# A compressing MLP whose first layer swaps its matmul operands, in a fused hybrid decoder block

## The chip, the cores and the metric

The kernel runs on one core of a Trainium2 chip. A core has a matrix engine (TensorE: PE in the rows, its weight loads PEld), a vector engine (VectorE, DVE), a scalar engine with function tables (ScalarE, ACT), GpSimd (POOL) and a queue that issues most DMAs (SyncE, SP). The metric is device time of one execution in microseconds (us), smaller being better. Of the kernel before, three runs gave 804.38, 804.61 and 807.77 us, a median of 804.61.

## The reference, cut to what matters

One decoder layer on 512 tokens of width 1024, all in float32: a norm, one input projection, four token mixers side by side, gates, an output projection, and an MLP. The change lies in the second mixer, sparse attention, and there in the small MLP that compresses keys and values:

```python
n_cmp = (S - CMP_LEN) // CMP_STRIDE + 1        # 31 windows of 32 tokens, 16 apart
def compress(t, pe, w1, w2):                    # t: keys or values, 2 heads of 64
    blk = jnp.take(heads(t), cmp_idx, axis=1) + pe[None, None, :, None, :]
    blk = jnp.swapaxes(blk, 2, 3).reshape(B, n_cmp, N_KV_HEADS, CMP_LEN * HEAD_DIM)
    hid = jax.nn.gelu(jnp.einsum('bnhf,fe->bnhe', blk, w1))   # f = 2048, e = 128
    return jnp.einsum('bnhe,ed->bnhd', hid, w2)               # d = 64
k_cmp = _rms(compress(kc, cmp_pe[0], cmp_w1[0], cmp_w2[0]), k_g[0])
v_cmp = compress(vc, cmp_pe[1], cmp_w1[1], cmp_w2[1])
```

So the first layer multiplies 62 rows (31 windows of 2 heads) of 2048 numbers by a weight of 2048 x 128, once for keys and once for values. Queries attend to `k_cmp`; the scores also choose the blocks that are read in full, and `v_cmp` is summed with them.

## The kernel before, in words

Activations lie transposed, features on the 128 partitions and tokens along the free dimension. A product of large matrices is split in three passes of a rounded type (`mm3`, lines 84 to 86: high by high, low by high, high by low), so PE runs long rows of matmuls of 128 x 128 weights against 256 or 512 columns. ACT makes the high half of each weight (line 79), DVE the low half (line 80).

Small pieces of attention are generators, called tasks. `tick()` steps at most two of them after each few matmuls of a projection, so their instructions are recorded between the projection's. The recorded program then goes through a scheduler that reorders the instructions of each engine by an estimate of its own; hence an edit in one task can move instructions far from it. On the chip each engine works off its queue in the order that results.

`cmp_task(j, acc)` compresses keys (j = 0) and values (j = 1). It loads `w1_j0` and `w1_j1` (two tiles of 8 weight blocks of 128 x 128), gathers windows into `blk_j` (128 x 16 x 62), and multiplies at line 544 in plain float32, 16 matmuls into one PSUM tile `hid_j`. A plain float32 matmul is two records in the trace, each with a weight load of its own. The weight block stays in the array (the stationary operand) and 62 columns of `blk` stream past it, so `hid_j` comes out as 128 hidden features x 62 windows. ACT applies gelu from PSUM into `hT0` (line 552) or, twice, into `hT1` (line 577), padded to 32 windows a head. Line 555 (`kcmp`) and line 580 (`vcmp`) multiply by the second layer's weight. From `kcmp` a norm on DVE and ACT makes `kccat`, line 571 turns it (`kctr`), and all attention heads wait for it and for `vcmp`.

All of this stands between the projections named `kv` (keys and values of the window), `gv` and `gu` (inputs of the gated mixer). After the changed place, PE also runs in half-width form, with 64 of the array's columns, for `gm` (line 720) and `pv` (lines 671 and 675), two such products beside each other.

The other names that the rows show: `VL` is gelu of `gv` (line 699); `rsu_k` a square root in a key's norm (line 356); `TG` tanh of attention gates (line 586); `kcat` and `KTT` a key before and after its turn (lines 492 and 74); `ktr` that turn (line 508); `s` the scores (lines 635 and 640); `p` their exponentials (line 648); `sh` and `gt` projections. ACT has one set of function tables at a time; where the next function belongs to another set, an ACT_TABLE_LOAD stands before it.

Of the kernel before, what the change touches and what calls it, by code (L numbers as in the profile page):

```python
# [11 lines left out]
AF = mybir.ActivationFunctionType  # L12
# [4 lines left out]
P = 128  # L17
# [8 lines left out]
NCMP = 31  # L26
# [11 lines left out]
def block_kernel(ctx: ExitStack, tc: tile.TileContext, x, w_in, w_branch, w_gate, w_out,  # L38
                 w_mlp1, w_mlp2, cmp_w1, cmp_w2, ws_t, bs, smalls, rows, norm1_g, norm2_g, out):
    nc = tc.nc  # L40
# [15 lines left out]
    def ps(name, dt=F32):  # L56
        return psp.tile([P, 512], dt, tag="ps", name=name)
# [7 lines left out]
    def t4(name, shape, dt=F32):  # L65
        return br.tile(shape, dt, tag="t4", name=name, bufs=8)

    def f32(ap):
        return ap.bitcast(F32)
# [263 lines left out]
    def rsqrt(dst, src, scale, eps, name, eng=None):  # L333
        ve = eng or nc.vector
        pr, n = src.shape[0], src.shape[1]
        h = const.tile([P, 16], F32, tag="rs_h", name=f"rsh_{name}", bufs=2)[:pr, :n]
        t = const.tile([P, 16], F32, tag="rs_t", name=f"rst_{name}", bufs=2)[:pr, :n]
        nc.vector.tensor_scalar(out=h, in0=src, scalar1=scale, scalar2=eps, op0=ALU.mult, op1=ALU.add)
        nc.vector.tensor_scalar(out=dst.bitcast(I32), in0=h.bitcast(I32), scalar1=-0.5, scalar2=float(0x5F3759DF),
                                op0=ALU.mult, op1=ALU.add)  # L340
        ve.tensor_scalar_mul(h, h, -0.5)
        for _ in range(3):
            ve.tensor_tensor(out=t, in0=dst, in1=dst, op=ALU.mult)
            ve.tensor_tensor(out=t, in0=t, in1=h, op=ALU.mult)
            if eng is None:
                ve.scalar_tensor_tensor(out=dst, in0=t, scalar=1.5, in1=dst, op0=ALU.add, op1=ALU.mult)
            else:
                ve.tensor_scalar_add(t, t, 1.5)
                ve.tensor_tensor(out=dst, in0=dst, in1=t, op=ALU.mult)
# [30 lines left out]
    ident = const.tile([P, P], F32, name="ident")  # L380
# [139 lines left out]
    def cmp_task(j, acc):  # L520
        w1 = []
        for half in range(2):
            w = t4(f"w1_{j}{half}", [P, 8, P])
            nc.sync.dma_start(w, cmp_w1[j, half * 1024 : (half + 1) * 1024, :].rearrange("(k p) c -> p k c", p=P))
            w1.append(w)
        kc = t4(f"kc_{j}", [P, S])
        nc.scalar.copy(kc, acc)
        kc2 = t4(f"kc2_{j}", [P, 2, S])
        nc.gpsimd.dma_start(kc2[0:64, 1, :], kc[64:128, :])
        nc.gpsimd.dma_start(kc2[64:128, 0, 0:511], kc[0:64, 1:512])  # L530
        nc.vector.tensor_copy(kc2[0:64, 0, :], kc[0:64, :])
        nc.vector.tensor_copy(kc2[64:128, 1, 0:511], kc[64:128, 1:512])
        blk = t4(f"blk_{j}", [P, 16, 2, NCMP])
        pe = sm[:, O_PE + 16 * j : O_PE + 16 * j + 16]
        for h in range(2):
            base = kc2[:, h, :].rearrange("p (n s) -> p s n", s=16)
            for u in range(2):
                nc.vector.tensor_tensor(
                    out=blk[:, 8 * u : 8 * u + 8, h, :], in0=base[:, 0:16:2, u : u + NCMP],
                    in1=pe[:, 8 * u : 8 * u + 8].unsqueeze(2).to_broadcast([P, 8, NCMP]), op=ALU.add)  # L540
        yield 9
        hp_ = ps(f"hid_{j}")
        for lp in range(16):
            nc.tensor.matmul(hp_[:, :62], w1[lp // 8][:, lp % 8, :], blk[:, lp, :, :].rearrange("p h n -> p (h n)"),
                             start=lp == 0, stop=lp == 15)
            if lp % 4 == 3 and lp < 15:
                yield 0
        hv = hp_[:, :62].rearrange("p (h n) -> p h n", h=2)
        if j == 0:
            hT = att.tile([P, 2, 32], F32, name="hT0")  # L550
            nc.gpsimd.memset(hT, 0.0)
            nc.scalar.activation(out=hT[:, :, :NCMP], in_=hv, func=AF.Gelu_apprx_tanh)
            yield 1
            kp = ps("kcmp")
            nc.tensor.matmul(kp[:64, :HD], hT.rearrange("p h n -> p (h n)"), w2[:, 0, :], start=True, stop=True)
            kr = att.tile([64, HD], F32, name="kr")
            nc.scalar.copy(kr, kp[:64, :HD])
            sq = kp[:64, :HD]
            nc.vector.tensor_tensor(out=sq, in0=kr, in1=kr, op=ALU.mult)
            ss = att.tile([64, 1], F32, name="kss")  # L560
            nc.vector.tensor_reduce(out=ss, in_=sq, axis=AX.X, op=ALU.add)
            r = att.tile([64, 1], F32, name="krr")
            rsqrt(r, ss, 1.0 / HD, 1e-6, "kc")
            nc.vector.scalar_tensor_tensor(out=kr, in0=kr, scalar=r[:, 0:1], in1=row[:64, R_KG : R_KG + HD],
                                           op0=ALU.mult, op1=ALU.mult)
            kk = att.tile([64, 2, HD], F32R, name="kccat")
            nc.scalar.copy(kk[:, 0, :], kr)
            nc.vector.tensor_tensor(out=kk[:, 1, :], in0=kr, in1=f32(kk[:, 0, :]), op=ALU.subtract)
            yield 4
            pt = ps("kctr", F32R)  # L570
            nc.tensor.transpose(pt[:, :64], kk.rearrange("p a d -> p (a d)"), identr[:64, :64])
            nc.vector.tensor_copy(KCT, f32(pt[:, :64]))
        else:
            hT = att.tile([P, 2, 2, 32], F32, name="hT1")
            nc.gpsimd.memset(hT, 0.0)
            for dup_ in range(2):
                nc.scalar.activation(out=hT[:, :, dup_, :NCMP], in_=hv, func=AF.Gelu_apprx_tanh)
            yield 1
            vp = ps("vcmp")
            nc.tensor.matmul(vp[:, :HD], hT.rearrange("p a b n -> p (a b n)"), w2[:, 1, :], start=True, stop=True)  # L580
            for h in range(4):
                nc.vector.tensor_copy(VBD[32 * h : 32 * h + 32, h, :], vp[32 * h : 32 * h + 32, :HD])
# [315 lines left out]
    for j in range(2):  # L898
        proj_T("kc", lambda j, a: tcmp.append(Task(cmp_task(j, a))), j)
# [576 lines left out]
```

## Time and profile before

| what | value |
|---|---|
| median of three runs | 804.61 us (804.38 to 807.77) |
| profiled execution, whole | 805.33 us |
| its span, first to last instruction | 803.4 us |
| PE busy | 792.0 us, 99% of the span |
| DVE, ACT, POOL busy | 607.3, 398.2, 91.2 us |
| granted TensorE clock | 1.00 in every stretch |

The profiled execution takes 1.9 us around its span. A busy PE counts records that overlap each other, so for the pace of a row of matmuls one reads the starts of records, not their lengths. In the timeline a row is: start, busy length, engine, line, operation, out<-in, shape, count; in brackets the idle time before it and what ended it.

### The profile page before, as it was taken

The page shows a single profiled execution, that of the slowest core. Times are in us where ns is not written, and L with a number is a line of the kernel's source. Part 1 is how long each engine was busy: PE and PEld are TensorE (multiplying, and loading weights), DVE is VectorE, ACT ScalarE, POOL GpSimd, SP SyncE. Part 2 cuts the span into 40 slices and gives each one's busy share as a digit, 9 for nine tenths or more (in the row PEclk, how much of TensorE's full clock was granted, in tenths as well). Part 3 has the DMA queues.
Part 4 walks back from the last instruction along what each step waited for, and adds up shares of the span by engine and source line. Part 5 has one row for each costly group of instructions (what it writes and reads, how often), then busy time and mean ns, then how long its engine had stood idle before and what let it go on. Part 6 is the DMA issues. An engine that isn't in the chain of part 4 may idle for free.

```text
span 803.4 us, 12441 instructions
## 1 busy us (share of the span) xinstructions
PE 792.0 (99%) x4985; PEld 697.2 (87%) x4985; DVE 607.3 (76%) x917; ACT 398.2 (50%) x625; POOL 91.2 (11%) x86
## 2 busy tenths in 40 slices
PE   7999999999999999999999999999999999999997
PEld 5989877777778788889998899889988998899987
DVE  5877873345999977848876679598879977997785
ACT  5646452443432424534565448534754475457642
POOL 6001011222313512221000010000000000000000
PEclk9999999999999999999999999999999999999999
DMA  9273223223122237212038252404241334233011
GB/s 303 70 195 99 66 65 94 79 79 80 55 65 66 79 119 221 73 60 77 30 106 287 80 161 89 145 27 139 85 145 53 109 103 138 71 106 105 27 53 53
DMA packets 93547, 81.47 MB, mean 101 GB/s; under 512 B 3921, under 2 KB 84849, under 8 KB 93490
## 3 DMA queue, kind: packets, MB, share of 16 engines
q1 hardware_dynamic: 91650, 74.51, 31.0%
q0 software_dynamic: 1120, 3.54, 1.4%
q10 hardware_dynamic: 720, 2.62, 0.9%
q8 instruction: 39, 0.64, 0.4%
q14 instruction: 18, 0.15, 0.1%
HBM read 78.05 MB, written 2.10 MB: 100 GB/s over the span
## 4 chain that ended last, share of the span: by engine, by line
PE 94%; DVE 2%; ACT 1%; DMA 1%; issue 0%; SPq 0%; ACTq 0%
PE gt L84 6%; PE gt L85 6%; PE gt L86 6%; PE o L84 4%; PE o L85 4%; PE o L86 4%; PE x_m L935 3%; PE x_m L937 3%; PE x_m L940 3%; PE pj L84 2%; PE pj L85 2%; PE pj L86 2%; PE wo L84 2%; PE wo L85 2%; PE wo L86 2%; PE pv L675 2%
## 5 line engine op out<-in xcount | busy, mean ns | idle before, releaser
L84 PE MATMUL gt<-XH,hi_wg 128*128 128x512 f32 x192 | 76.4, 398 | 0.0
L86 PE MATMUL gt<-XH,lo_wg 128*128 128x512 f32 x192 | 75.9, 395 | 0.0
L85 PE MATMUL gt<-XL,hi_wg 128*128 128x512 f32 x192 | 75.6, 394 | 0.0
L653 POOL TENSOR_SCALAR p<-p,c 128x128 f32<-128x128 f32 (+3 forms) x32 | 42.8, 1350 | 144.7 <-DVE c L651 130.6
L85 PE MATMUL o<-lo_m,hd 128*128 128x512 f32 x128 | 50.6, 395 | 0.0
L79 ACT CAST hi_wg<-raw_wg 128x1024 fp32r<-128x1024 f32 x24 | 25.1, 1047 | 49.8 <-PE gt L85 28.9
L86 PE MATMUL o<-hi_m,hd 128*128 128x512 f32 x128 | 48.0, 394 | 0.0
L743 DVE SCALAR_TENSOR_TENSOR cv<-Z,sm,cv 128x512 f32<-128x512 f32 x60 | 47.7, 820 | 0.3
L84 PE MATMUL o<-hi_m,hd 128*128 128x512 f32 x128 | 47.3, 396 | 0.1
L80 DVE TENSOR_TENSOR lo_pm<-rawg_m,hi_pm 128x1024 fp32r<-128x1024 f32 x28 | 34.2, 1223 | 12.7 <-ACT hi_pm L79 12.7
L86 PEld LDWEIGHTS gt<-XH,lo_wg 128*128 128x128 f32 x192 | 36.1, 188 | 8.4
L85 PEld LDWEIGHTS gt<-XL,hi_wg 128*128 128x128 f32 x192 | 36.1, 188 | 8.3 <-issue 0.3
L84 PEld LDWEIGHTS gt<-XH,hi_wg 128*128 128x128 f32 x192 | 36.1, 188 | 7.9 <-issue 0.2
L80 DVE TENSOR_TENSOR lo_wg<-raw_wg,hi_wg 128x1024 fp32r<-128x1024 f32 x24 | 29.3, 1220 | 16.5 <-ACT hi_wg L79 16.4
L937 PE MATMUL x_m<-T,hi_pm 128*128 128x256 f32 x168 | 41.6, 280 | 0.0
L935 PE MATMUL x_m<-T,hi_pm 128*128 128x256 f32 x168 | 41.6, 281 | 0.0
L79 ACT CAST hi_pm<-rawg_m 128x1024 fp32r<-128x1024 f32 x28 | 29.4, 1050 | 22.6 <-PE x_m L937 9.5
L80 DVE TENSOR_TENSOR lo_pm<-sg_m,hi_pm 128x1024 fp32r<-128x1024 f32 x21 | 25.7, 1223 | 18.8 <-ACT hi_pm L79 18.8
L1351 PE MATMUL ox<-hi_po,hd 128*128 128x256 f32 x128 | 36.0, 281 | 0.8 <-DVE X L1364 0.8
L80 DVE TENSOR_TENSOR hd<-R,hd 128x1024 fp32r<-128x1024 f32 x28 | 34.1, 1220 | 3.3 <-ACT hd L79 3.3
L990 POOL TENSOR_TENSOR MIX<-MIX,g 128x512 f32<-128x512 f32 x16 | 26.5, 1662 | 88.0 <-DVE g L989 86.8
L1353 PE MATMUL ox<-lo_po,hd 128*128 128x256 f32 x128 | 36.1, 282 | 0.0
(502 smaller groups left out, 2520.6 us busy)
## 6 DMA issues: line engine op xcount, KB each, us to landing
raw_wg<-in_w_gate_dram SPq DMA_DIRECT2D x24, 512.0 KB, 4.2
rawg_m<-in_w_mlp_dram SPq DMA_DIRECT2D x24, 512.0 KB, 3.8
raw_m<-in_w_mlp_dram SPq DMA_DIRECT2D x20, 512.0 KB, 4.1
rawg_o<-in_w_mlp_dram SPq DMA_DIRECT2D x16, 512.0 KB, 4.1
raw_wb<-in_w_branch_dram SPq DMA_DIRECT2D x16, 256.0 KB, 2.6
rawg_g<-in_w_gate_dram SPq DMA_DIRECT2D x8, 512.0 KB, 5.7
raw_wo<-in_w_out_dram SPq DMA_DIRECT2D x8, 512.0 KB, 3.6
x<-in_x_dram SPq DMA_DIRECT2D x4, 512.0 KB, 6.9
```

What stands on the lines that cost most here:

```text
L79: i = nc.scalar.copy(hi, src)
L80: (eng or nc.vector).tensor_tensor(out=lo, in0=src, in1=f32(hi), op=ALU.subtract)
L84: nc.tensor.matmul(dst, l[0], r[0], start=start, stop=False)
L85: nc.tensor.matmul(dst, l[0], r[1], start=False, stop=False)
L86: nc.tensor.matmul(dst, l[1], r[0], start=False, stop=stop)
L653: nc.gpsimd.tensor_scalar_mul(p_[:, b, :w], p_[:, b, :w], c2[:, b : b + 1])
L743: nc.vector.scalar_tensor_tensor(out=cv[:, j, :], in0=Z[:, j, k : k + S], scalar=wc, in1=cv[:, j, :], op0=ALU.mult, op1=ALU.add)
L935: nc.tensor.matmul(acc[:, p, :], hi[:, kk, sl], th[:, kk, :], start=kk == 0 and p == 0 and n in (1, 2, 5), stop=False, skip_group_check=True)
L937: nc.tensor.matmul(acc[:, p, :], hi[:, kk, sl], tl[:, kk, :], start=False, stop=False, skip_group_check=True)
L990: (nc.vector if last else nc.gpsimd).tensor_tensor(out=mx, in0=mx, in1=gt, op=ALU.add)
L1351: nc.tensor.matmul(acc[:, p, :], th[:, kk, sl], hi[:, kk, :], start=kk == 0 and p == 0 and n in (1, 2, 5), stop=False, skip_group_check=True)
L1353: nc.tensor.matmul(acc[:, p, :], th[:, kk, sl], lo[:, kk, :], start=False, stop=False, skip_group_check=True)
```

## The change

At line 544 the operands trade places. The 62 columns of `blk` become the stationary operand, the 128 columns of a `w1` block stream past, and `hid_j` comes out as 62 windows x 128 features. ACT applies gelu once per j, on 62 partitions x 128, into the first weight block of `w1_j0`, which is no longer needed. PE turns that by a transpose against the identity (62 x 128 to 128 x 62) into another part of the same PSUM tile, and DVE copies the turned values to `hT0`, or twice to `hT1`, where ACT wrote gelu before.

```diff
         for lp in range(16):
-            nc.tensor.matmul(hp_[:, :62], w1[lp // 8][:, lp % 8, :], blk[:, lp, :, :].rearrange("p h n -> p (h n)"),
+            nc.tensor.matmul(hp_[:62, :P], blk[:, lp, :, :].rearrange("p h n -> p (h n)"), w1[lp // 8][:, lp % 8, :],
                              start=lp == 0, stop=lp == 15)
             if lp % 4 == 3 and lp < 15:
                 yield 0
-        hv = hp_[:, :62].rearrange("p (h n) -> p h n", h=2)
+        hg = w1[0][:62, 0, :]
+        nc.scalar.activation(out=hg, in_=hp_[:62, :P], func=AF.Gelu_apprx_tanh)
+        yield 1
+        nc.tensor.transpose(hp_[:, P : P + 62], hg, ident[:62, :62])
+        hv = hp_[:, P : P + 62].rearrange("p (h n) -> p h n", h=2)
         if j == 0:
             hT = att.tile([P, 2, 32], F32, name="hT0")
             nc.gpsimd.memset(hT, 0.0)
-            nc.scalar.activation(out=hT[:, :, :NCMP], in_=hv, func=AF.Gelu_apprx_tanh)
+            nc.vector.tensor_copy(hT[:, :, :NCMP], hv)
...
             for dup_ in range(2):
-                nc.scalar.activation(out=hT[:, :, dup_, :NCMP], in_=hv, func=AF.Gelu_apprx_tanh)
+                nc.vector.tensor_copy(hT[:, :, dup_, :NCMP], hv)
```

The scheduler also moves other instructions, from this place until some 325 us into the span; behind that all engines have the order of before. From line 556 on a line's number is 4 higher after the change: `VL` is line 703, `kcmp` 559, `kctr` 575, `vcmp` 584, the scores 639.

The first place, on PE, is where values are compressed and `kcmp` follows the keys' gelu. `gv_0` and `gv_1` are projections of 128 tokens each. Before:

```order
L86 MATMUL gv_0_978<-hi_gv1_966,XL_134 128x256
L555 MATMUL kcmp_991<-w2_129,hT0_950 64x64
L544 MATMUL hid_1_1017<-blk_1_777,w1_10_766 128x62 x8
L508 MATMUL ktr1_0_1038<-identr_110,kcat_k10_881 128x128 x2
L544 MATMUL hid_1_1017<-blk_1_777,w1_11_768 128x62 x3
L84 MATMUL gv_1_1042<-hi_gv0_782,XH_133 128x256
```

After the change, the same place from the turn of the keys (line 551) on:

```order
L551 MATMUL hid_0_874<-ident_100,w1_00_704 128x62
L85 MATMUL gv_0_976<-lo_gv1_965,XH_133 128x256
L86 MATMUL gv_0_976<-hi_gv1_964,XL_134 128x256
L84 MATMUL gv_0_976<-hi_gv1_964,XH_133 128x256
L85 MATMUL gv_0_976<-lo_gv1_965,XH_133 128x256
L86 MATMUL gv_0_976<-hi_gv1_964,XL_134 128x256
L544 MATMUL hid_1_993<-w1_10_766,blk_1_777 62x128 x4
L544 MATMUL hid_1_993<-w1_11_768,blk_1_777 62x128 x5
L559 MATMUL kcmp_1010<-w2_129,hT0_990 64x64
L84 MATMUL gv_1_1040<-hi_gv0_782,XH_133 128x256
```

`kcmp` stood ahead of the values' first matmul and now stands behind the thirteenth (four more stand ahead of the first row shown); it joins their half-width stretch, and the last three follow behind `gv_1`.

The second place is ACT from `kr`, the copy of `kcmp`, to the values' gelu. Before:

```order
L557 COPY kr_993<-kcmp_991 64x64
L356 ACT_TABLE_LOAD
L356 ACTIVATE rsu_k12_1060<-rsv_k12_1059 128x2
L74 CAST KTT_137<-ktr1_0_1038 128x2x128
L356 ACTIVATE rsu_k13_1151<-rsv_k13_1150 128x2
L586 ACT_TABLE_LOAD
L586 ACTIVATE TG_140<-TG_140 128x48
L492 CAST kcat_k12_1134<-hraw_k12_929 128x2x64
L567 CAST kccat_1014<-kr_993 64x64
L699 ACT_TABLE_LOAD
L699 ACTIVATE VL_965<-gv_1_1042 128x256
```

After:

```order
L356 ACT_TABLE_LOAD
L356 ACTIVATE rsu_k12_1079<-rsv_k12_1078 128x2
L74 CAST KTT_137<-ktr1_0_1057 128x2x128
L703 ACT_TABLE_LOAD
L703 ACTIVATE VL_963<-gv_1_1040 128x256
L356 ACT_TABLE_LOAD
L356 ACTIVATE rsu_k13_1167<-rsv_k13_1166 128x2
L590 ACT_TABLE_LOAD
L590 ACTIVATE TG_140<-TG_140 128x48
L492 CAST kcat_k12_1145<-hraw_k12_929 128x2x64
L549 ACT_TABLE_LOAD
L549 ACTIVATE w1_10_766<-hid_1_993 62x128
```

`VL` of `gv_1` moved between the two square roots, so five table loads instead of three stand between `kr` and the values' gelu (line 549; before, two instructions behind the last row shown).

The third place, on PE, is the values' turn and what is queued behind it, after the change:

```order
L84 MATMUL gv_2_1087<-hi_gv1_964,XH_133 128x256
L551 MATMUL hid_1_993<-ident_100,w1_10_766 128x62
L85 MATMUL gv_2_1087<-lo_gv1_965,XH_133 128x256
L86 MATMUL gv_2_1087<-hi_gv1_964,XL_134 128x256
L639 MATMUL s_00_1530<-KTT_137,QT0_135 128x256
L639 MATMUL s_00_1530<-KTT_137,QT1_136 128x256
L639 MATMUL s_01_1550<-KTT_137,QT0_135 128x256
L639 MATMUL s_01_1550<-KTT_137,QT1_136 128x256
L575 MATMUL kctr_1121<-identr_110,kccat_1033 128x64
L584 MATMUL vcmp_1124<-w2_129,hT1_1101 128x64
L84 MATMUL gv_3_1130<-hi_gv0_782,XH_133 128x256
```

The turn (line 551) is new; before, nothing on PE needed the values' gelu until `vcmp`, which stood one matmul ahead of the end of `gv_2`.

Over the whole program the stretches in which PE is not in its full 128 x 128 form number 32 before and 38 after. Before: one at the start, `kcmp`, `kctr`, 5 of `gm` and 24 of `pv`. After: one at the start, 7 of line 544 (4 for keys with 8 records each; 3 for values with 8, 18 and 6, `kcmp` inside the second), 2 turns, `kctr`, 5 of `gm` and 22 of `pv`. ACT's table loads number 11 before and 15 after.

## Rows read from the trace of the kernel before

**Rows 1.** The page: busy time by engine, and the chain that ended last by engine

```profile
PE 792.0 (99%) x4985; PEld 697.2 (87%) x4985; DVE 607.3 (76%) x917; ACT 398.2 (50%) x625; POOL 91.2 (11%) x86
PE 94%; DVE 2%; ACT 1%; DMA 1%; issue 0%; SPq 0%; ACTq 0%
```

**Rows 2.** Busy time in the stretch around the change, with clock and DMA

```profile
60.00:100.00 40.00, 40.00 (x292) 36.41 (x291) 31.11 (x154) 20.74 (x45) 5.51 (x9) 1.00 0.30 83
```

**Rows 3.** Waits of PE's weight loads, 60 to 110 us: total, times, longest

```profile
PEld kcmp L555 <- ACT hT L552: 0.2, 1, 0.2
```

**Rows 4.** The first layer's records: ns min/median/max, first and last start

```profile
L544 PE MATMUL hid<-blk,w x64: 216/275/322, 62.2 to 79.9; 128*128 128x62 f32 x64
```

**Rows 5.** Timeline of PE, one stretch of the first layer between `kv`

```profile
62.11 0.28 PE L86 MATMUL kv<-hi_kv,XL 128*128 128x256 f32 x1
62.23 1.00 PE L544 MATMUL hid<-blk,w 128*128 128x62 f32 x8
63.04 0.36 PE L84 MATMUL kv<-hi_kv,XH 128*128 128x256 f32 x1
63.24 0.28 PE L85 MATMUL kv<-lo_kv,XH 128*128 128x256 f32 x1
```

**Rows 6.** Timeline of PE, one float32 product in half-width form

```profile
204.56 0.39 PE L85 MATMUL sh<-XL,hi_sh 128*128 128x512 f32 x1
204.79 0.40 PE L86 MATMUL sh<-XH,lo_sh 128*128 128x512 f32 x1
205.12 0.43 PE L675 MATMUL pv<-pT,V 128*64 128x128 f32 x2
205.48 0.51 PE L84 MATMUL sh<-XH,hi_sh 128*128 128x512 f32 x1
205.82 0.39 PE L640 MATMUL s<-KTT,QT 128*128 128x512 f32 x1
```

**Rows 7.** Timeline of PE, fifteen such products, eight in one half

```profile
255.72 1.96 PE L675 MATMUL pv<-pT,V 128*64 128x128 f32 x30
```

**Rows 8.** Timeline of PE around `kctr`, a turn of 64 rows

```profile
81.36 0.28 PE L86 MATMUL gv<-hi_gv,XL 128*128 128x256 f32 x1
81.57 0.25 PE L571 MATMUL kctr<-identr,kccat 64*128 64x64 f32 x1
81.75 0.38 PE L84 MATMUL gv<-hi_gv,XH 128*128 128x256 f32 x1
81.97 0.28 PE L85 MATMUL gv<-lo_gv,XH 128*128 128x256 f32 x1
```

**Rows 9.** Timeline of ACT from the keys' gelu to `VL`

```profile
71.49 1.28 ACT L552 ACT_TABLE_LOAD   x1
72.78 0.22 ACT L552 ACTIVATE hT<-hid 128x62 f32<-128x62 f32 x1
72.90 0.28 ACT L471 ACTIVATE kv<-hraw_k 128x128 f32<-128x128 f32 x1
...
73.43 0.21 ACT L557 COPY kr<-kcmp 64x64 f32<-64x64 f32 x1
...
74.94 0.20 ACT L356 ACTIVATE rsu_k<-rsv_k 128x2 f32<-128x2 f32 x1
75.51 0.37 ACT L74 CAST KTT<-ktr 128x256 fp32r<-128x256 f32 x1 [0.36 <-PE ktr L508]
...
77.69 0.24 ACT L586 ACTIVATE TG<-TG 128x48 f32<-128x48 f32 x1
77.84 0.28 ACT L492 CAST kcat_k<-hraw_k 128x128 fp32r<-128x128 f32 x1
...
80.13 0.38 ACT L699 ACTIVATE VL<-gv 128x256 f32<-128x256 f32 x1
```

**Rows 10.** Timeline of PE: the second layer's matmul of the keys

```profile
73.06 0.33 PE L555 MATMUL kcmp<-w,hT 128*64 128x64 f32 x2
```

**Rows 11.** ACT's wait in the stretch of `gu`: total, times, longest

```profile
ACT hi_wb L79 <- PE gu L85: 6.3, 1, 6.3
```

## The prediction

> **What bounds the kernel now.** I read the shares of the page first: PE is busy for 99% of the span, and the chain that ended last is PE for 94% [rows 1]. The stretch around the change says the same more sharply: of 40 us PE is busy for 40.0, at a granted clock of 1.00 (its 2.4 GHz level), while DVE has 9 us to spare and ACT 19 [rows 2]. Then I read PE's waits there: the only one that names gelu is `kcmp`'s for `hT`, 0.2 us [rows 3]. So the kernel is one queue of matmuls. An edit costs what it adds to PE's row of starts, and what it makes PE wait; work on ACT and DVE counts only where PE comes to wait for it.
>
> **The matmuls themselves.** The 32 first-layer matmuls are 64 records before and after [rows 4]. Before, eight of them and two `kv` starts take 63.24 - 62.23 = 1.01 us; less one `kv` pace of 0.12 (62.23 - 62.11) that leaves 0.111 us a record [rows 5]. With 62 columns streaming, that pace belongs to the load of 128 columns of weights rather than to the stream. After, 62 columns are loaded and 128 stream past. `pv` is just that form, with 64 columns. A lone product (2 records) is busy 0.43 us [rows 6]; a row of 30 has 16 in one half of the array and 14 in the other, and is busy 1.96 us [rows 7]: (1.96 - 0.43) / 14 = 0.109 us for each further record of one half. At that pace the 64 records cost 64 x (0.109 - 0.111) = -0.1; I take **-0.1**. Twice the columns streaming and half the columns loaded cancel out.
>
> Here a rule of the Trainium skill promises more. "TensorE: Matmul & The Clock Gate", section "LDWEIGHTS (loading the stationary operand)", lets the load's time grow with its columns; estimated from it, 62 columns load in 52 ns where 128 take 107. If the load alone set the pace, it would halve. The `pv` rows, with 64 columns, do not show half the pace, so the trace disagrees with that reading for 128 streaming columns.
>
> **Leaving the full form.** A stretch with 64 of the columns has a price at both ends. From the last full matmul ahead of a lone `pv` product to the second one behind it, starts stand 205.82 - 204.79 = 1.03 us apart; two full ones at 204.79 - 204.56 = 0.23 and two records at 0.109 would make 0.68. A round trip costs 0.35 us [rows 6]. Line 544 was in the full form and paid none: its eight records fit at 0.111 each with both ends in the sum. Now it makes seven stretches, and one takes in `kcmp`, which had a trip of its own: 6 more, 6 x 0.35 = **+2.1**. (`pv` stands between 512-column matmuls, line 544 between 256-column ones; I take the same price.)
>
> **The two turns.** `kctr` is a turn of 64 rows between full matmuls: from 81.36 to 81.97 is 0.61 us where two full ones at 0.12 take 0.24, so one turn costs 0.37 [rows 8]. Two are new: **+0.7**.
>
> **Trips saved by the new order.** Behind the change 22 stretches of `pv` stand where 24 did: 2 x 0.35 = **-0.7**. And `kcmp`'s 0.2 us of waiting goes, since nine matmuls of values now stand between the keys' turn and it: **-0.2**. They cover the DVE copy too, which is not on PE's row. The keys' gelu is not late for its turn either. Before, it ended at 73.0 [rows 9]; PE was at `kcmp` at 73.06 [rows 10], 72.9 without the wait, and gets to the turn with five `gv` fewer (0.6), eight records (0.9) and five trips (1.75) more ahead of it, at some 74.9.
>
> **The wait that is added.** The second turn needs the values' gelu, and ACT gets there late. Before, three table loads stood between `kr` and that gelu, and PE needed nothing of it until `vcmp`. After, five do. I add up ACT's queue from `kcmp`'s start, with durations of [rows 9, 10]: `kr` starts 0.37 behind it (73.43 - 73.06); `kr` 0.21, `rsu_k` 0.20 twice, `KTT` 0.37, `VL` 0.38, `TG` 0.24, `kcat` 0.28, and the new gelu, bounded by 0.22 (62 columns) and 0.38 (256) and taken as 0.28 from the 128-column row: 2.2 us. Five loads at 1.28 are 6.4. Together 9.0. Each of the loads is followed by its function without a gap (71.49 + 1.28 = 72.77, gelu at 72.78), so nothing more is added. PE has, from `kcmp` to the turn: 46 `gv` at 0.12 = 5.5, `kcmp`'s two records with the way out of half width some 0.4, two `ktr` pairs some 0.3 (a turn's pace taken as a `gv`'s at most), six records with a trip 0.65 + 0.35 = 1.0: 7.2 us. PE stands still for 9.0 - 7.2 = **+1.8**. Behind the turn wait the rest of `gv_2`, the first scores, `kctr` and `vcmp`, and with them everything.
>
> A page speaks for a still longer wait. By "ScalarE: Activation LUTs", section "What ACT_TABLE_LOAD costs", a switch is a load of 1283 ns and a drain of 1380. The row agrees on the load and shows no drain; by the page's sum the five switches would add 6.9 us, and the kernel would take some 815. No chance is given to that.
>
> **What follows from ACT and DVE being later.** `vcmp` waits for two DVE copies that start behind the turn, and the first `gm` for norms of `VL`, which ACT delivers behind one more load. The trace of before has neither wait. Below, nothing; above, a whole load on the path, 1.28. I take **+0.4**, nearer to nothing since between the turn and that `gm` PE has 24 matmuls of `gv_3` (2.9 us) and 24 of `gu_0` at 0.23 (5.5). The two other new loads stand around the second half of `GU`, where ACT idled for 6.3 us [rows 11]: nothing.
>
> **Sum:** -0.1 + 2.1 + 0.7 - 0.7 - 0.2 + 1.8 + 0.4 = +4.0 us. On the profiled execution's own time that is 805.33 + 4.0 = 809.3. The median of the runs is 0.7 below that execution, so I predict 804.6 + 4.0, with the roundings 808.5 us, 0.5% slower; this lies on the border of what a measurement of this kernel can tell from no change (about 0.5%, 4.0 us).
>
> **Rivals.**
>
> *The loads were the price, and it halves.* If the 0.109 of `pv` comes from loads for both halves of the array at once and a lone half could go at half of it, 64 records save 64 x 0.054 = 3.5 us, of which 0.3 lie under ACT's wait. For it: two halves' loads do share those rows. Against it: the last, unpaired product of [rows 7] keeps the pace. Time: 808.5 - 3.2 = 805.3. Chance 8%.
>
> *In one half, loads are not hidden.* Line 544 uses one half alone, where `pv` alternates. The lone `pv` product's two records start 0.43 - 0.27 = 0.16 us apart (0.27 being a record's length by the median of [rows 4]). If each record pays that rather than only the first, 0.05 more on 51 records (of the 64, seven first steps are counted in the trip and six lie under ACT's wait) is 2.6 us: 811.1, slower by 0.8%. It decides from 0.002 us a record on, since the sum lies so near the border. Against it: the same [rows 7], where no step behind the first is so long. Chance 14%.
>
> By the section "The mechanism" of "TensorE: Matmul & The Clock Gate" (in its list of what overlaps), a weight load overlaps a running matmul only where the row group differs, which would make this rival the rule; [rows 5], where full-array `kv` loads vanish behind a pace of 0.12, contradict it.
>
> *The second turn does not wait.* ACT reaches the values' gelu in time, because PE is late for reasons of its own, or `VL` comes sooner: 808.5 - 1.8 = 806.7. For it: the 1.8 is a difference of two sums of 9.0 and 7.2. Against it: five loads alone are 6.4. Chance 12%.
>
> **How the numbers follow.** My forecast holds 66%, with a range of its own of 807.0 to 810.2 (the later waits at 0 or 1.28, the trip at 0.3 to 0.4). With the rivals the range that should hold 8 in 10 is 805.6 to 811.2. Slower by over 0.5% (808.6 on): nearly half of the forecast's share and all of the second rival's, 0.44. Within 0.5%: the rest of the forecast, nearly all of the first and third rival's, 0.52. Faster: 0.04, for a new order that saves what I don't see.
>
> **What would show it.** In the profile after: line 544 with records 0.109 us apart within a stretch and 0.35 a trip; PE's wait for gelu at line 551, one of near 1.8 us and one of nothing; 15 table loads, five between `kr` and the values' gelu; behind 325 us the same row of PE, shifted. A pace of 0.05 or 0.16, no wait at the turn, or a wait of PE at a place not named here, in the heads or in the branches behind them, would make it wrong.

## The result, and the profile after

The changed kernel takes 810.1 us (median of 8 runs, 809.4 to 815.4) beside 804.6 us for the kernel before: a ratio of 1.0071, 95% interval 1.0044 to 1.0099. It is slower by 5.5 us where 4.0 were forecast. Some executions of either kernel take about 3 us or more longer; in the profiled run of the changed kernel, which is one of them (813.0 us, span 811.3), the time is lost in the first 25 us, where PE waits for the first weights, and without such executions the medians are 809.5 and 804.4, 5.1 us apart.

So the two traces are first set side by side by the starts of the same instructions. Below are rows of the view by tile: count, nanoseconds min/median/max, first and last start in us, form. First the kernel before (its `hid` row is [rows 4]), then the changed one.

```profile
L84 PE MATMUL gu<-XH,hi_gu x16: 392/398/505, 87.0 to 99.9; 128*128 128x512 f32 x16
L1351 PE MATMUL oz<-hi_po,th x32: 277/280/284, 533.3 to 784.2; 128*128 128x256 f32 x32
```

```profile
L544 PE MATMUL hid<-w,blk x64: 272/273/322, 65.0 to 84.6; 128*62 128x128 f32 x64
L84 PE MATMUL gu<-XH,hi_gu x16: 387/398/498, 95.6 to 107.4; 128*128 128x512 f32 x16
L1355 PE MATMUL oz<-hi_po,th x32: 277/281/284, 541.3 to 792.1; 128*128 128x256 f32 x32
```

At the first `hid` matmul the changed kernel is 65.0 - 62.2 = 2.8 us behind, before the change has done anything. At `gu` it is 95.6 - 87.0 = 8.6 behind, so the change has cost 5.8 by then; at the first `oz` 541.3 - 533.3 = 8.0, which leaves 5.2. All of the loss lies between 65 and 96 us, and 0.6 comes back in the stretch of the heads. Behind that, nothing moves.

In that stretch the profile after reads as follows. The windows have the length, the busy time of PE, PEld, DVE, ACT and POOL, the granted clock of PE, and two columns on DMA.

```profile
60.00:100.00 40.00, 38.17 (x274) 34.57 (x274) 25.69 (x116) 22.33 (x46) 4.64 (x8) 0.96 0.24 67
```

[Rows 2] had PE busy for 40.00 of 40 us at a clock of 1.00. Now 1.8 us of idle time stand there, and the clock is below 1. PE's waits (total, times, longest) name the idle time; the last row is a wait at 102 us that the change brought on top of it:

```profile
PE hid L551 <- ACT w L549: 1.7, 1, 1.7
PE gm L724 <- DVE rst_ln L344: 0.3, 1, 0.3
```

The same place in short windows shows where the clock went:

```profile
86.00:88.00 2.00, 1.88 (x17) 1.67 (x15) 0.35 (x4) 1.94 (x6) 0.00 (x0) 1.00 0.00 0
88.00:90.00 2.00, 0.39 (x2) 0.33 (x3) 1.66 (x16) 1.68 (x3) 0.00 (x0) 1.00 0.00 0
90.00:91.00 1.00, 1.00 (x7) 0.76 (x6) 1.00 (x12) 0.30 (x2) 0.00 (x0) 0.82 0.00 0
91.00:94.00 3.00, 2.90 (x14) 2.89 (x14) 2.93 (x16) 0.28 (x1) 0.00 (x0) 0.50 0.00 0
94.00:96.00 2.00, 2.00 (x17) 1.95 (x16) 1.30 (x8) 1.61 (x2) 0.00 (x0) 0.99 0.00 0
```

PE stands idle in 88 to 90, at a clock that still reads 1.00. Behind the wait the granted clock is 0.50, the lower of its two levels (1.2 GHz): for 3.4 us, from 90.64 (0.82 is the mean of 90 to 91) to some 94.04. PE is at work for almost all of it: a slow clock does not show as idle time. It shows in the distance of starts. The timeline of PE (start, duration, instruction, in brackets the idle time ahead and its releaser):

```profile
87.60 0.28 PE L84 MATMUL gv<-hi_gv,XH 128*128 128x256 f32 x1
89.61 0.27 PE L551 MATMUL hid<-ident,w 62*128 62x62 f32 x1 [1.73 <-ACT w L549]
...
90.73 0.31 PE L575 MATMUL kctr<-identr,kccat 64*128 64x64 f32 x1
91.14 0.66 PE L584 MATMUL vcmp<-w,hT 128*128 128x64 f32 x2
91.92 0.41 PE L85 MATMUL gv<-lo_gv,XH 128*128 128x256 f32 x1
...
93.84 0.38 PE L85 MATMUL gv<-lo_gv,XH 128*128 128x256 f32 x1
94.05 0.29 PE L86 MATMUL gv<-hi_gv,XL 128*128 128x256 f32 x1
94.17 0.28 PE L84 MATMUL gv<-hi_gv,XH 128*128 128x256 f32 x1
```

From 91.92 to 94.05 ten `gv` starts follow each other at 0.213 us; from 94.05 on it is 0.12 again, as in [rows 5]. That is 10 x 0.093 = 0.93 us. From `kctr` to 91.92 it is 1.19 us; the same three steps take some 0.6 at full clock (0.18 behind `kctr` in [rows 8], 0.25 and 0.19 behind `vcmp` in the profile of the fourth experiment below). Together 1.5 us that no view lists as a wait.

### The profile page after: what moved, and what is told of

Its sections match the earlier page's. It is cut to its first block, busy times and chain, and to the rows that moved or that the text cites. A ratio compares the mean times of both kernels' runs of the same rounds, so it can differ in the third digit from the quotient of the medians.

```text
span 811.3 us, 12445 instructions
## 1 busy us (share of the span) xinstructions
PE 795.9 (98%) x4987; PEld 700.0 (86%) x4987; DVE 608.7 (75%) x920; ACT 405.0 (50%) x628; POOL 97.6 (12%) x86
## 4 chain that ended last, share of the span: by engine, by line
PE 92%; DVE 3%; ACT 3%; DMA 1%; issue 0%; SPq 0%; ACTq 0%
PE gt L84 6%; PE gt L86 6%; PE gt L85 5%; PE o L84 4%; PE o L85 4%; PE o L86 4%; PE x_m L939 3%; PE x_m L941 3%; PE x_m L944 3%; PE pj L84 2%; PE pj L86 2%; PE pj L85 2%; PE wo L84 2%; PE wo L85 2%; PE wo L86 2%; PE z_m L941 2%
## 5 line engine op out<-in xcount | busy, mean ns | idle before, releaser
L86 PE MATMUL gt<-XH,lo_wg 128*128 128x512 f32 x192 | 75.9, 395 | 0.0
L657 POOL TENSOR_SCALAR p<-p,c 128x128 f32<-128x128 f32 (+3 forms) x32 | 48.2, 1517 | 157.1 <-DVE c L655 138.2
L86 PE MATMUL o<-hi_m,hd 128*128 128x512 f32 x128 | 48.1, 394 | 0.0
L747 DVE SCALAR_TENSOR_TENSOR cv<-Z,sm,cv 128x512 f32<-128x512 f32 x60 | 45.5, 786 | 0.3
L86 PEld LDWEIGHTS gt<-XH,lo_wg 128*128 128x128 f32 x192 | 36.1, 188 | 8.6 <-issue 0.2
```

The source lines that it names most:

```text
L86: nc.tensor.matmul(dst, l[1], r[0], start=False, stop=stop)
L657: nc.gpsimd.tensor_scalar_mul(p_[:, b, :w], p_[:, b, :w], c2[:, b : b + 1])
L747: nc.vector.scalar_tensor_tensor(out=cv[:, j, :], in0=Z[:, j, k : k + S], scalar=wc, in1=cv[:, j, :], op0=ALU.mult, op1=ALU.add)
```

## The experiments

Three theories. *T*: the wait at the turn costs its 1.7 us and, by the clock behind it, 1.5 more. *F*: the half-width form brings the clock down, wait or no wait. *N*: the clock is no cost; the missing 1.5 us are trips that are dearer than 0.35. Times are medians; the kernel before is run beside each group. What is called a step in some of the expectations is a change between full and half height or width in PE's order of instructions; two steps are a trip. Counted in the traces, the kernel before has 63 steps and the changed one 75. The scheduler orders the heads anew with every edit, so each experiment's count stands with it; it bears on how a difference is read.

**A late turn (e1_late_turn).** `lastmm` holds the last `L86` matmul; `issue_after` keeps an instruction behind it on its engine.

```diff
-        yield 1
-        nc.tensor.transpose(hp_[:, P : P + 62], hg, ident[:62, :62])
+        yield 1 if j == 0 else 3
+        with tc.issue_after(lastmm[0].ins):
+            nc.tensor.transpose(hp_[:, P : P + 62], hg, ident[:62, :62])
...
-            yield 4
+            yield 5
             pt = ps("kctr", F32R)
-            nc.tensor.transpose(pt[:, :64], kk.rearrange("p a d -> p (a d)"), identr[:64, :64])
+            with tc.issue_after(lastmm[0].ins):
+                nc.tensor.transpose(pt[:, :64], kk.rearrange("p a d -> p (a d)"), identr[:64, :64])
```

> The changed kernel with the second turn, and the key block's turn behind it, put some fifteen matmuls later, into the last gv projection, so that ScalarE has written the activated values before TensorE comes to them. Theory T (the 1.7 us wait costs itself and, behind it, 3 us of matmuls at half the clock, 1.5 us): no wait of TensorE at the second L551, granted clock 1.00 in every stretch from 85 to 100 us, and both terms gone: 5.1 - 1.7 - 1.5, about 2 us above the kernel before, 806.5 us. Rival F (the half-width stretches and turns bring the clock down, whether TensorE waits or not): the 0.50 stays somewhere behind the turn, about 3.5 above, 808. Rival N (the clock in the record is no cost; the missing 1.5 us are trips at more than 0.35): 3.4 above, 808.

806.23 us beside 804.36, ratio 1.0029 (1.0013 to 1.0046). PE waits for nothing at the second turn, and the windows where it now stands (it starts at 89.56 in this profile) read:

```profile
88.00:90.00 2.00, 1.94 (x15) 1.62 (x13) 1.66 (x16) 1.91 (x4) 0.00 (x0) 1.00 0.00 0
90.00:92.00 2.00, 2.00 (x16) 1.88 (x16) 2.00 (x19) 1.39 (x3) 0.00 (x0) 1.00 0.00 0
```

The half-width form of the first layer is all there, and the clock is 1.00: F falls. Of the 5.5 us some 3.6 are gone. Not all of that is the wait and the clock behind it: this order has 71 steps, two trips fewer, and the 0.3 at `gm` is gone as well. By T 1.7 + 1.5 + 0.6 + 0.3 = 4.1 should have gone. By N, whose trips cost (2.1 + 1.5) / 6 = 0.6, it is 1.7 + 1.2 + 0.3 = 3.2. So this run does not decide between T and N.

**Full rows (e2_full_rows).** The stationary operand is 128 columns wide, of which the product uses 62.

```diff
-        blk = t4(f"blk_{j}", [P, 16, 2, NCMP])
+        bf = t4(f"blk_{j}", [P, 1084])
+        nc.gpsimd.memset(bf[:, 992:1058], 0.0)
+        blk = bf[:, :992].rearrange("p (l h n) -> p l h n", l=16, h=2)
...
-            nc.tensor.matmul(hp_[:62, :P], blk[:, lp, :, :].rearrange("p h n -> p (h n)"), w1[lp // 8][:, lp % 8, :],
+            nc.tensor.matmul(hp_[:, :P], bf[:, 62 * lp : 62 * lp + P], w1[lp // 8][:, lp % 8, :],
```

> The changed kernel with a stationary operand of 128 columns instead of 62 (the 66 more are the next pair's tokens or zeros, and the rows of the sum that they make are not read), so that the sixteen matmuls of each half are of the form of their neighbours; order of operands, activation, turn and its wait stay. Theory T: the six more half-width trips, 6 x 0.35 = 2.1 us, go; the wait of 1.7 to 2.1 at the second turn and the half clock behind it stay: about 3 us above the kernel before, 807.5. Rival F: clock 1.00 throughout, about 1.5 above, 806. Rival N (more than 0.35 for a trip): all but 0.7 + 1.7 gone, 2.4 above, 807.

807.96 us, ratio 1.0040 (1.0025 to 1.0055), nearest to T. It has 63 steps, as the kernel before, so the trips net out of the 3.6 us that it takes more. N expected 2.4, and only 0.3 of the rest is the wait, which is 2.0 us here. Without any half-width matmul in the first layer the clock falls behind it (a row of the waits, then windows):

```profile
PE hid L553 <- ACT w L551: 2.0, 1, 2.0
```

```profile
84.00:86.00 2.00, 0.96 (x6) 0.90 (x7) 1.66 (x15) 1.11 (x3) 0.00 (x0) 0.91 0.00 0
86.00:88.00 2.00, 2.00 (x10) 1.71 (x10) 2.00 (x14) 0.58 (x2) 0.00 (x0) 0.50 0.00 0
88.00:90.00 2.00, 2.00 (x14) 2.00 (x14) 1.93 (x12) 0.27 (x1) 0.00 (x0) 0.74 0.00 0
```

Nine of the 12 runs are at 807.5 to 810.4 with a mean clock of 0.996 to 0.998, three at 806.6 to 806.8 with 0.999 or 1.000.

**Both edits together (e3_full_rows_late).**

> Both edits, the 128-column stationary operand and the late second turn. Left of the change are the swapped operands, two turns at 0.37 and their place. All theories: within 1 us of the kernel before, 804.6 to 805.6, since the form, the wait and what the clock takes are all gone. If the swapped operands cost in themselves (a slower record, a weight load that is not hidden), 2 us or more stay although no half-width trip and no wait is left.

804.41 us, ratio 0.9997 (0.9980 to 1.0014). Nothing is left of the 5.5 us, though operands are still swapped and both turns are there. With 59 steps, two trips fewer than the kernel before, and a wait of 0.3 at the second turn (row below), it should lie some 0.3 under it; that it doesn't stays open. From the late turn in half width to this one it is 806.23 - 804.41 = 1.8 us for six trips, 0.3 a trip, or 0.35 with that wait taken out. N needs 0.6, and falls.

```profile
PE hid L555 <- ACT w L552: 0.3, 1, 0.3
```

**A wait alone, in the kernel before (e4_wait_alone).** The edit puts five times the same useless activation, of another table, ahead of the values' gelu, which overwrites what it wrote (the added line is shown once).

```diff
+            nc.scalar.activation(out=hT[:, :, 0, :NCMP], in_=hv, func=AF.Tanh)
             for dup_ in range(2):
                 nc.scalar.activation(out=hT[:, :, dup_, :NCMP], in_=hv, func=AF.Gelu_apprx_tanh)
-            yield 1
```

> The kernel before, its operands as they were and no turn, with a wait alone: five useless activations with another table ahead of the values' gelu, and the step between the gelu and the matmul vcmp taken out, so that TensorE stands at vcmp for about 1.8 us. Theory T: a full-height kernel too falls to half the clock behind such a wait, for about 3 us, and its gv_3 and gu_0 stand 1.7 + 1.5 = 3.2 us later than in the kernel before; some of it may come back where the heads are ordered anew: 1.5 to 3.5 us above, 806 to 808. Rivals F and N: clock 1.00 behind the wait, gv_3 1.7 us later and no more; 0.5 to 1.7 above.

806.28 us, ratio 1.0011 (0.9994 to 1.0027), but the runs lie on two levels. Five are at 804.5 to 805.1 with a mean clock of 0.999 or 1.000; six are at 806.2 to 806.7, all with 0.998; one is at 809.3 with 1.000. The profiled run is of the lower level. Its wait stands there, and behind it `gv` goes on at 0.12:

```profile
81.06 0.43 PE L584 MATMUL vcmp<-w,hT 128*128 128x64 f32 x2 [1.60 <-ACT hT L582]
81.31 0.37 PE L84 MATMUL gv<-hi_gv,XH 128*128 128x256 f32 x1
81.50 0.28 PE L85 MATMUL gv<-lo_gv,XH 128*128 128x256 f32 x1
81.62 0.28 PE L86 MATMUL gv<-hi_gv,XL 128*128 128x256 f32 x1
```

The lower level is only 0.2 us above the kernel before, with a wait of 1.6: taking `yield 1` out also moved the heads, and at 55 steps four trips fewer give back 1.2.

So this one program has executions in which the clock falls and others in which it doesn't, 1.9 us apart (medians 804.6 and 806.5). No trace of the upper level was kept; that the clock falls behind this wait there is inferred from the next experiment's trace. That is T's price, at full width and without a turn, but T as I wrote it expected it in every run. The profile alone could not have shown it; the list of all runs with their clocks did. Three more lengths of the same wait followed.

**A longer wait (e5_wait_long).** Two activations of two other tables (tanh, exp) in place of the five.

> As e4_wait_alone (the kernel before, operands as they were, no turn, a wait alone at vcmp), but with two useless activations of two other tables, which keep ScalarE some 1.5 us longer, and so TensorE: a wait of about 3.5 us. In e4 the runs lay on two levels, five at 804.5 to 805.1 with a mean clock of 0.999 to 1.000 and six at 806.2 to 806.7 with 0.998, and the one profiled was of the upper clock. If the wait is what brings the clock down, and a longer one does so more surely: half clock for some 3 us behind vcmp in the profiled run, a mean clock of 0.998 in every run, time 2 us (what the wait adds) and 1.8 us (the distance of the two levels in e4) above the kernel before: 808. If something else made the two levels of e4 (chance, another place): clock 1.00 behind the wait, two levels again, the lower at 806.3.

809.2 us (five runs), ratio 1.0056 (1.0043 to 1.0068), every run with a clock of 0.995 to 0.998: three at 809.2 to 809.3 with 0.995 or 0.996, two at 807.9 and 808.1 with 0.998. The wait, and the windows behind it:

```profile
PE vcmp L581 <- ACT hT L579: 3.4, 1, 3.4
```

```profile
80.00:82.00 2.00, 0.00 (x0) 0.00 (x0) 1.59 (x10) 1.97 (x3) 0.00 (x0) 0.87 0.00 0
82.00:84.00 2.00, 1.04 (x5) 1.04 (x6) 0.30 (x2) 1.97 (x4) 0.00 (x0) 0.50 0.00 0
84.00:86.00 2.00, 2.00 (x11) 2.00 (x10) 1.28 (x8) 1.97 (x6) 0.00 (x0) 0.50 0.00 0
86.00:88.00 2.00, 2.00 (x11) 1.71 (x11) 1.20 (x10) 0.33 (x1) 0.15 (x1) 0.50 0.00 0
88.00:90.00 2.00, 2.00 (x17) 2.00 (x17) 1.34 (x7) 0.39 (x1) 1.31 (x2) 0.92 0.00 0
```

Here the low clock begins while PE still stands idle, and lasts for some 5 us of its work. This is the kernel before with its own operands and without the new turns; the wait was added, and the heads' order came out with 57 steps, three trips fewer. An estimate from these rows: 3.4 of wait, less 0.9 for the trips, and 5 us at 0.213 a start in place of 0.12, which lose 2.2, make 4.7 of the 5.0 us above the kernel before. The time is 1.2 above what I expected, since the low stretch is longer than the 3 us that I carried over from the changed kernel.

**A wait of 1.9 us (e6_wait_2us)**, six such activations in place of five.

> As e4_wait_alone with one more useless activation, 0.28 us: a wait of 1.9 us in place of 1.6. If the length of the wait decides how often the clock falls: most runs on the upper level, 806.5 to 807, and few on the lower, 804.8. If it doesn't: about half on each, as in e4.

804.75 us, ratio 1.0012 (1.0003 to 1.0021). Six runs at 804.4 to 804.8 with a clock of 0.999 or 1.000, five at 805.9 to 806.3 with 0.997 or 0.998. Not "most on the upper level": between 1.6 and 1.9 us the length does not decide. The steps are 55 again.

**A wait of 1.1 us (e7_wait_1us)**, three of them.

> As e4_wait_alone with two useless activations fewer: a wait of about 1.1 us. If the length decides: all runs on the lower level, at 804.0 to 804.6, mean clock 0.999 or 1.000. If it doesn't: two levels, the upper 1.8 us above the lower.

803.96 us, ratio 1.0000 (0.9991 to 1.0009); all eleven runs have a clock of 0.999 or 1.000, as expected. With 55 steps here too, the 1.2 of four trips cover the wait, so the time does not rise at all.

**A still later turn (e8_later_turn).** As the late turn, but `yield 6` in place of 3, and `kctr` where its step puts it.

> The changed kernel, half-width form and all, with the second turn still later than in e1_late_turn (behind the whole gv projection), the key block's turn where its step puts it, and nothing that TensorE waits for. It has 67 steps between full and half height on TensorE where the kernel before has 63, after 75 and e1 71. If the cost of the change is trips, wait and clock: 2 trips of 0.35 more than before and no wait, 804.5 to 805.5, under e1 by 0.7 or more; the clock 1.00 from 75 to 110 us. If something of the swapped operands is left that no trip or wait explains: 806 as e1.

809.09 us, ratio 1.0064 (1.0051 to 1.0077): a miss. The count of 67 steps in the expectation was wrong; the program has 77. And the wait had only moved, to the next instruction that needs ScalarE:

```profile
PE kctr L577 <- DVE kccat L574: 1.4, 1, 1.4
PE gm L726 <- DVE rsh_ln L339: 0.6, 1, 0.6
```

The timeline of ACT in the same run says why. `kccat` stands right behind the values' gelu, and both behind a table load (each row: start, duration, instruction):

```profile
86.05 1.28 ACT L550 ACT_TABLE_LOAD   x1
87.35 0.27 ACT L550 ACTIVATE w<-hid 62x128 f32<-62x128 f32 x1
87.52 0.23 ACT L573 CAST kccat<-kr 64x64 fp32r<-64x64 f32 x1
```

The clock stayed at 1.00 in all five runs. Waits of 1.4 and 0.6, and seven trips more than the kernel before at 0.3, make 4.1 of the 4.9 us; 0.8 stays open.

**The turn first, the activation behind it (e9_turn_first).** VectorE copies the raw sum for the turn, and ScalarE's gelu writes `hT` as in the kernel before.

```diff
-        nc.scalar.activation(out=hg, in_=hp_[:62, :P], func=AF.Gelu_apprx_tanh)
+        nc.vector.tensor_copy(hg, hp_[:62, :P])
...
-            nc.vector.tensor_copy(hT[:, :, :NCMP], hv)
+            nc.scalar.activation(out=hT[:, :, :NCMP], in_=hv, func=AF.Gelu_apprx_tanh)
...
-                nc.vector.tensor_copy(hT[:, :, dup_, :NCMP], hv)
+                nc.scalar.activation(out=hT[:, :, dup_, :NCMP], in_=hv, func=AF.Gelu_apprx_tanh)
```

> The changed kernel with the activation behind the turn: VectorE copies the sum from PSUM, TensorE turns it, and ScalarE writes hT from the turned sum as in the kernel before; half-width form and turns stay. If the 1.7 us wait is ScalarE's queue of five table loads (and not the turn itself): no wait of TensorE at L551, at most some 0.7 us at vcmp, which now is the first to need the values' gelu, and, with e7_wait_1us as the measure of a wait so short, clock 1.00 from 85 to 100 us. Left are six trips and two turns, 2.1 + 0.7, and that wait: 806.3 to 807.5. If the turn itself holds TensorE up: 809 as the changed kernel.

807.29 us, ratio 1.0042 (1.0029 to 1.0054). No wait at L551, 0.6 us at `vcmp`, clock 0.999 or 1.000 in all runs: the turn itself holds nothing up; ScalarE's queue does. With 77 steps, seven trips more at 0.3 and the wait make 2.7 of the 3.0 us.

**The same with full rows (e10_turn_first_full)**, and `vcmp` behind an anchor.

> As e9_turn_first, with the 128-column stationary operand of e2_full_rows and vcmp some steps later, so that nothing is waited for and nothing but the two turns is of half height. Two turns at 0.37 above the kernel before, less the two trips of pv that are gone, as in e3_full_rows_late: 804.0 to 805.2.

804.05 us, ratio 0.9998 (0.9990 to 1.0007), again level with the kernel before. Against the run above that is 3.2 us: 0.6 of wait and 18 steps, nine trips at 0.29.

**The kernel before, with two places moved (e11_before_later).** `yield 4` ahead of `kctr` becomes 9, `yield 1` ahead of `vcmp` 7.

> The kernel before with its operands as they were, and the key block's turn and vcmp each some steps later. The place of these two sets in which order the heads run beside the gates, and so how often TensorE goes between full and half height: 53 steps where the kernel before has 63, five trips less at 0.3 to 0.35, against a wait of 0.5 us for GU. If trips are what the heads' order costs: 1.0 to 1.2 us under the kernel before, 803.0. If the order doesn't matter: 804.2 to 804.7.

803.25 us, ratio 0.9985 (0.9977 to 0.9994): 1.1 us below the kernel before, the only version here whose interval lies below it. It swaps no operands; by its order of instructions (53 steps) it saves five trips, and PE waits 0.3 us for `GU` on the way.

## Why the prediction was right, and where it fell short

The time lies inside the range (805.6 to 811.2), 1.6 above the forecast. In part that is luck: the upper bound stems from the second rival, whose pace of 0.16 us the trace does not show, and the forecast's own range to 810.2 is wider than the two terms it names make it. Later waits of 1.28 in place of 0.4, and four trips net at 0.4 in place of 0.35, give 808.5 + 0.9 + 0.2 = 809.6, under the measured 810.1. The terms one by one:

- **The records, -0.1: right.** To the next full matmul, eight records take 66.01 - 65.00 = 1.01 us (rows of the next point) and six 84.83 - 84.04 = 0.79. So a further record is 0.11 us, neither 0.055 (the first rival) nor 0.16 (the second): both fall.

```profile
84.04 0.87 PE L544 MATMUL hid<-w,blk 128*62 128x128 f32 x6
84.83 0.38 PE L84 MATMUL gv<-hi_gv,XH 128*128 128x256 f32 x1
```

- **Six trips, +2.1: right, the size perhaps a little high.** Between `kv` starts a stretch of eight takes 66.23 - 64.79 = 1.44 us, and 63.24 - 62.11 = 1.13 in [rows 5]; the difference is 0.31, and the pairs of experiments give 0.29 to 0.35. So six trips cost 1.7 to 2.1.

```profile
64.79 0.28 PE L86 MATMUL kv<-hi_kv,XL 128*128 128x256 f32 x1
65.00 1.08 PE L544 MATMUL hid<-w,blk 128*62 128x128 f32 x8
66.01 0.38 PE L84 MATMUL kv<-hi_kv,XH 128*128 128x256 f32 x1
66.23 0.28 PE L85 MATMUL kv<-lo_kv,XH 128*128 128x256 f32 x1
```

- **Two turns, +0.7: right.** The first one, with no wait at it, takes 77.99 - 77.36 = 0.63 where two `gv` steps take 0.24: 0.39, against 0.37 from [rows 8].

```profile
77.36 0.28 PE L84 MATMUL gv<-hi_gv,XH 128*128 128x256 f32 x1
77.57 0.27 PE L551 MATMUL hid<-ident,w 62*128 62x62 f32 x1
77.77 0.38 PE L85 MATMUL gv<-lo_gv,XH 128*128 128x256 f32 x1
77.99 0.28 PE L86 MATMUL gv<-hi_gv,XL 128*128 128x256 f32 x1
```

- **The wait at the second turn, +1.8: right**, at 1.73 us, by the mechanism named. ACT's `kr` starts at 80.88 and the values' gelu at 89.29, with five loads of 1.28 between; 15 loads in all, where the kernel before has 11. No load is followed by a pause: 87.99 + 1.28 = 89.27.

```profile
80.88 0.20 ACT L561 COPY kr<-kcmp 64x64 f32<-64x64 f32 x1 [1.84 <-PE kcmp L559]
...
87.99 1.28 ACT L549 ACT_TABLE_LOAD   x1
89.29 0.27 ACT L549 ACTIVATE w<-hid 62x128 f32<-62x128 f32 x1
```

- **Later waits, +0.4: right**, 0.3 at the first `gm`.
- **Trips of `pv` that are gone, -0.7:** 0.6 of the lag comes back between `gu` and `oz`, and 0.3 is lost there at `gm`, so 0.9 in all. That these trips are what gives it back was not tried alone.

The step that failed is in the same paragraph as the wait: "Behind the turn wait the rest of `gv_2`, the first scores, `kctr` and `vcmp`, and with them everything." It prices a wait of PE at its own length. Behind this one the clock was at half for 3.4 us, and the matmuls that came next took 1.5 us more. Summed up to `gu` the prediction's terms give 2.1 - 0.1 + 0.7 - 0.2 + 1.8 = 4.3, and the trace has 5.8: the difference is the clock, to within 0.1. The evidence on which I left it out was a stretch that had no wait in it: [rows 2] show 1.00 for a PE that is never idle, which says nothing of a PE that is. My three rivals all changed the size of a cost already in the sum; none added the clock to it.

That the wait brings the clock down is shown from both sides: without the wait the half-width kernel keeps 1.00, and with a wait alone the kernel before loses it. The price is shown too: 1.9 us between the two levels of the fourth experiment, 1.5 between those of the sixth (medians 804.5 and 806.0), 1.5 in the rows above. Since the sum stood at the border of 0.5%, those 1.5 us carried the time over it.

The Trainium skill's page "TensorE: Matmul & The Clock Gate", section "What's actually happening", says that a hardware monitor sets the clock by how busy the array has lately been, and that the number of slow matmuls differs from run to run of one kernel (its figures are from a kernel's start). The two levels agree with that: 6 of 12 runs at 0.998 for a wait of 1.6 us, 5 of 11 at 0.997 or 0.998 for 1.9. Why, with 1.7 us, all 8 runs of the changed kernel have a mean clock of 0.995 to 0.998 stays open; only one has a trace, and what runs ahead of the wait differs (a last half-width stretch and `gv`, where the kernel before has full-width records and scores).

## What to carry to other kernels

Where one engine bounds the kernel, a wait put into its row costs its own length and can cost as much again in the clock behind it; the second part shows as busy time, so look at the granted clock in short windows behind each new wait, and at the clocks of all runs, not of the profiled one alone. Swapping operands was free here record by record: what cost was leaving the form of the neighbours (0.3 us a trip), and a stationary operand of 128 columns, of which 62 are used, took that away at a cost that these runs, which leave some 0.3 us open, don't show. An edit that adds a wait can also give the work behind it another order: count what that saves before reading a difference of a microsecond. A result that PE needs back should not come through the engine whose queue is full of table loads; let an engine with slack copy it, and do the activation behind the turn (here the wait fell from 1.7 to 0.6 us).

## What the runs showed of the hardware that I had not expected

- The same program, with the same wait of 1.6 us, is 1.9 us faster or slower by whether the clock falls behind it (mean granted clock 0.999 to 1.000, or 0.998). By the mean clocks it fell behind 1.1 us in none of 11 runs and behind 1.4 us (the later turn) in none of 5, behind 2.0 us (full rows) in 9 of 12, and behind 3.4 us in all of 5.
- In the first 25 us of the changed kernel's profile PE waits 1.8 us for `lo_q`, and the clock in 18 to 22 us is 0.62; in the profile of the late turn the same wait of 1.8 us is followed by 1.00.

```profile
18.00:22.00 4.00, 4.00 (x24) 4.00 (x24) 0.97 (x3) 1.63 (x3) 1.81 (x1) 0.62 0.87 246
```

```profile
18.00:22.00 4.00, 4.00 (x24) 4.00 (x24) 0.42 (x2) 0.83 (x2) 1.88 (x1) 1.00 0.84 243
```

- A weight load of 62 columns is 135 ns and one of 128 columns 192 ns in the rows of PEld (line 544 of the changed kernel, and of the kernel before), and yet the matmuls keep one pace, 0.11 us a record.
